# A two-layer transformer trunk: pairs of up-projection tiles as seven block products, and weight sums made by adding transfers

## The chip, the cores and the metric

The kernel runs on one core of a Trainium2 chip. The time is the device time of one execution in microseconds (us); less is better. The kernel before took 1202.36 us (median of three runs, 1201.91 to 1202.77).

The engines of the core are named as the profile names them: PE is TensorE (matmuls), PEld its weight loads, DVE is VectorE, ACT is ScalarE, POOL is GpSimd and SP is SyncE, which here only issues transfers. Each engine runs its own queue of instructions in order and waits on semaphores for what others have to finish first.

## The reference

x has 512 tokens of 1024 features. Each of two layers mixes tokens (an mLSTM in the first, pooling in the second), attends to a memory of 256 tokens, and ends with a squared-ReLU MLP of 4096 hidden features. The change touches only the MLP:

```python
ALPHA = (2 * DEPTH) ** 0.25                    # DEPTH = 2
def sq_relu_mlp(x, w1, b1, w2, b2):
    return jnp.square(jax.nn.relu(x @ w1 + b1)) @ w2 + b2
...
for i in range(DEPTH):
    ...
    x = layer_norm(ALPHA * x + sq_relu_mlp(x, mlp_w1[i], mlp_b1[i], mlp_w2[i], mlp_b2[i]),
                   ln_g[i, 2], ln_b[i, 2])
```

All of it is float32.

## The kernel before

**Split products.** Every float32 operand is kept as a high part (a copy rounded to the matmul's own float32 form) and a low part (what the rounding left). `mm3` (L196) makes one product of three matmuls: high by high, high by low, low by high. The parts of a weight tile are made by `unit` (L160, L161): ACT casts the raw 128x1024 tile to `wh`, DVE subtracts `wh` from it and writes `wl`. The pools hold five `wh`, five `wl` and eight large activation tiles.

**The MLP** goes in four quarters q of 1024 hidden features. In each, the up projection makes eight tiles h of 128 features by 512 tokens. `feat_tile` (L299) makes one of them with 8 x 3 matmuls that stream 512 columns of xm (the normalised x, transposed; `xm00h` and `xm01h` are the high parts of its first and last 512 features in layer 0, `xm10h` and `xm11h` in layer 1). `feat_first` (L287) makes the first four of q = 0 in two rounds of 256 columns, so that they can begin while the last tokens are still being normalised. ACT turns each tile into relu (r, L809) and its square (s, L810).

For q = 0, 1 and 2 `up_down` (L799) makes the down projection as seven block products instead of eight (Strassen's scheme in Winograd's form): the hidden features are cut into four blocks a11, a21, a12, a22, the weights into b11, b12, b21, b22; sums of blocks are formed, split into parts (`split`, L777 and L778; `weight_split`, L786 and L787), and `product` multiplies them in the PSUM banks u, f and m2. After each product `onto` (L845) adds a bank to x or subtracts it. `each` (L833) forms the weight sums t1, t2, t3, t4 on DVE, 128x1024 at a time. Just after `feat_first`, x is scaled and b2 is added (L820). Quarter q = 3 is done plainly.

**Order.** The program is written in the order of the code, and a list scheduler of the framework then orders the instructions of each engine by its own costs. Each engine runs its queue in that order.

Of the kernel before, what the change touches and what calls it, by code (L numbers as in the profile page):

```python
# [19 lines left out]
KC = D // P  # L20
# [13 lines left out]
SUM = sum(SEG)  # L34
WU = 1024
LN_T = 7.2


def f32(ap):
    return ap.bitcast(F32)  # L40
# [3 lines left out]
def trunk(ctx: ExitStack, tc: tile.TileContext, a: dict, out: bass.AP):  # L44
    nc = tc.nc
    V, A, G, T = nc.vector, nc.scalar, nc.gpsimd, nc.tensor
# [5 lines left out]
    act_p = pool("act", 8)  # L52
    wh_p = pool("wh", 5)
    wl_p = pool("wl", 5)
# [14 lines left out]
    scoped = {}  # L69
# [20 lines left out]
    def ld(dst, src):  # L90
        nc.sync.dma_start(dst, src)
# [561 lines left out]
    for i in range(DEPTH):  # L653
# [120 lines left out]
        def split(name, src):  # L774

            h, l = [scoped["hid"].tile([P, 4, 256], F32R, tag="hid", name=f"{name}{p}") for p in "hl"]
            A.copy(h, src)  # L777
            V.tensor_tensor(l, src, f32(h), ALU.subtract)  # L778
            return h, l

        def weight_split(name, src):
            us = []
            for j, r in enumerate(src):
                h = wh_p.tile([P, WU], F32R, tag="wh", name=f"{name}h{j}")
                l = wl_p.tile([P, WU], F32R, tag="wl", name=f"{name}l{j}")
                A.copy(h, r)  # L786
                V.tensor_tensor(l, r, f32(h), ALU.subtract)  # L787
                us.append([z.rearrange("p (k m) -> p k m", m=512) for z in (h, l)])
            return us

        def product(ps, lhs, rhs, start, evac):

            for g in range(2):
                for k in range(4):
                    w = rhs[k // 2]
                    mm3(ps[g], tuple(z[:, k, tok(g)] for z in lhs), (w[0][:, k % 2], w[1][:, k % 2]), start=start and k == 0, stop=k == 3, skip=not start)
                evac(g, ps[g])

        def up_down(q, n):  # L799
# [25 lines left out]
            def load(name, hf, j, z=None):  # L825
                z = z or [scoped["rawd"].tile([P, WU], F32, tag="rawd", name=f"{name}{n}{z}") for z in range(2)]
                for w in range(2):
                    ld(z[w], a["w2"][i, q, hf, j + w])
                return z

            def each(dst, x_, y_, op):
                for d, u, v in zip(dst, x_, y_):
                    V.tensor_tensor(d, u, v, op)  # L833

            for m in range(first, KC):
                ev(m, feat_tile(f"h{n}{m}", a["w1"][i, 8 * q + m], xm, aux_p, "aux"))
                if m == 3 or m == first == 4:
                    L["M1"] = split(f"a11{n}", a11)
                    V.tensor_tensor(a11, a11, a21, ALU.subtract)
                    L["M7"] = split(f"q3{n}", a11)  # L840
# [12 lines left out]
            b11 = load("b11", 0, 0)  # L853
            product(u, L["M1"], weight_split(f"b11{n}", b11), True, onto(0, 0))
            b12 = act_p.tile([P, 2, WU], F32, tag="act", name=f"b12{n}")
            b12 = load("b12", 1, 0, [b12[:, w] for w in range(2)])
            each(b11, b11, b12, ALU.add)
            V.tensor_tensor(a21, a21, a22, ALU.subtract)
            product(f, split(f"q1{n}", a21), weight_split(f"t1{n}", b11), True, onto(1, 1))
            b22 = load("b22", 1, 2)  # L860
            V.scalar_tensor_tensor(a11, a11, -1.0, a22, ALU.mult, ALU.subtract)
            each(b11, b11, b22, ALU.add)
            product(u, split(f"q2{n}", a11), weight_split(f"t2{n}", b11), False, onto(0, 1, ALU.subtract))
            b21 = load("b21", 0, 2)
            product(m2, split(f"a12{n}", a12), weight_split(f"b21{n}", b21), True, onto(0, 0))
            each(b12, b12, b22, ALU.add)
            product(u, L["M7"], weight_split(f"t3{n}", b12), False, onto(1, 1, ALU.subtract))
            V.tensor_tensor(a12, a12, a11, ALU.add)
            product(f, split(f"q4{n}", a12), weight_split(f"b22{n}", b22), False, onto(0, 1))
            each(b11, b11, b21, ALU.add)  # L870
            product(u, split(f"a22{n}", a22), weight_split(f"t4{n}", b11), False, onto(1, 0))

        for q in range(3):
            up_down(q, f"{i}{q}")
# [110 lines left out]
```

## Time and profile before

| of the profiled execution | |
|---|---|
| its own time | 1203.3 us |
| span from the first to the last instruction | 1201.2 us |
| PE busy | 1189.4 us, 99% of the span |
| DVE busy | 812.6 us, 68% |
| ACT busy | 575.5 us, 48% |
| mean granted TensorE clock | 0.998 of full speed |
| bytes moved | 146.58 MB |

The execution's own time is 2.1 us over its span. A matmul's row gives its length from start to modelled end; matmuls overlap, so what one costs is read from the distance between two starts. A letter such as `h<-xm00h,wh` means: writes h, reads xm00h and wh; the numbers of tiles are left out in rows of the trace. In the rows of the program's order the tile's own number stands behind its name: `h003` is feature tile 3 of layer 0, quarter 0, and `a1100h` is the high part of block a11 of layer 0, quarter 0.

### The profile page before, as it was taken

The page shows a single profiled execution, that of the slowest core. Times are in us where ns is not written, and L with a number is a line of the kernel's source. Part 1 is how long each engine was busy: PE and PEld are TensorE (multiplying, and loading weights), DVE is VectorE, ACT ScalarE, POOL GpSimd, SP SyncE. Part 2 cuts the span into 40 slices and gives each one's busy share as a digit, 9 for nine tenths or more (in the row PEclk, how much of TensorE's full clock was granted, in tenths as well). Part 3 has the DMA queues.
Part 4 walks back from the last instruction along what each step waited for, and adds up shares of the span by engine and source line. Part 5 has one row for each costly group of instructions (what it writes and reads, how often), then busy time and mean ns, then how long its engine had stood idle before and what let it go on. Part 6 is the DMA issues. An engine that isn't in the chain of part 4 may idle for free.

```text
span 1201.2 us, 15360 instructions
## 1 busy us (share of the span) xinstructions
PE 1189.4 (99%) x6105; PEld 1013.5 (84%) x6105; DVE 812.6 (68%) x1089; ACT 575.5 (48%) x832; POOL 19.1 (2%) x51
## 2 busy tenths in 40 slices
PE   9999999999999999999999999999999999999997
PEld 6888899889888988888888888998988888888886
DVE  6764466585549685693884598874968569388336
ACT  6685775224423553454545434552355445454530
POOL 0211000000000000000000000000000000000000
PEclk9999999999999999999999999999999999999999
DMA  7244257633243306125025355635231513502311
GB/s 270 95 136 123 88 158 263 199 100 107 70 162 101 124 21 207 53 99 181 1 67 216 123 193 176 185 115 175 88 123 39 189 53 118 163 1 73 103 53 70
DMA packets 44056, 146.58 MB, mean 122 GB/s; under 512 B 5568, under 2 KB 5836, under 8 KB 43984
## 3 DMA queue, kind: packets, MB, share of 16 engines
q1 hardware_dynamic: 42960, 142.96, 36.2%
q0 software_dynamic: 1024, 2.64, 1.0%
q8 instruction: 48, 0.79, 0.3%
q14 instruction: 24, 0.20, 0.0%
HBM read 139.27 MB, written 6.31 MB: 121 GB/s over the span
## 4 chain that ended last, share of the span: by engine, by line
PE 94%; DVE 2%; ACT 1%; DMA 1%; issue 0%; SPq 0%; DVEq 0%; ACTq 0%
PE h L198 10%; PE h L197 10%; PE h L199 10%; PE u L197 4%; PE u L198 4%; PE u L199 4%; PE m L197 3%; PE m L199 3%; PE m L198 3%; PE ao L199 2%; PE ao L197 2%; PE ao L198 2%; PE q L197 2%; PE q L198 2%; PE q L199 2%; PE f L199 2%
## 5 line engine op out<-in xcount | busy, mean ns | idle before, releaser
L161 DVE TENSOR_TENSOR wl<-raw,wh 128x1024 fp32r<-128x1024 f32 x175 | 213.3, 1221 | 194.0 <-ACT wh L160 192.0
L160 ACT CAST wh<-raw 128x1024 fp32r<-128x1024 f32 x175 | 183.3, 1050 | 286.5 <-PE h L198 92.1
L833 DVE TENSOR_TENSOR b<-b,b 128x1024 f32<-128x1024 f32 x48 | 57.6, 1220 | 0.4
L197 PE MATMUL h<-xm10h,wh 128*128 128x512 f32 (+1 forms) x144 | 52.8, 367 | 0.0
L197 PE MATMUL h<-xm00h,wh 128*128 128x512 f32 (+1 forms) x144 | 52.8, 367 | 0.0
L197 PE MATMUL h<-xm01h,wh 128*128 128x512 f32 (+1 forms) x144 | 52.8, 367 | 0.0
L197 PE MATMUL h<-xm11h,wh 128*128 128x512 f32 (+1 forms) x144 | 52.8, 367 | 0.0
L198 PE MATMUL h<-xm00l,wh 128*128 128x512 f32 (+1 forms) x144 | 52.7, 366 | 0.0
L198 PE MATMUL h<-xm10l,wh 128*128 128x512 f32 (+1 forms) x144 | 52.7, 366 | 0.0
L199 PE MATMUL h<-xm01h,wl 128*128 128x512 f32 (+1 forms) x144 | 52.6, 365 | 0.0
L199 PE MATMUL h<-xm10h,wl 128*128 128x512 f32 (+1 forms) x144 | 52.6, 365 | 0.0
L199 PE MATMUL h<-xm11h,wl 128*128 128x512 f32 (+1 forms) x144 | 52.6, 365 | 0.0
L199 PE MATMUL h<-xm00h,wl 128*128 128x512 f32 (+1 forms) x144 | 52.6, 365 | 0.0
L198 PE MATMUL h<-xm01l,wh 128*128 128x512 f32 (+1 forms) x144 | 52.6, 365 | 0.0
L198 PE MATMUL h<-xm11l,wh 128*128 128x512 f32 (+1 forms) x144 | 52.6, 365 | 0.0
L809 ACT ACTIVATE r<-h,b 128x512 f32<-128x512 f32 x48 | 32.8, 683 | 14.8 <-PE h L199 14.8
L248 ACT ACTIVATE rs<-mv,eps_t 128x1 f32<-128x1 f32 x24 | 7.1, 294 | 53.3 <-DVE mv L246 53.3
L810 ACT ACTIVATE s<-r 128x512 f32<-128x512 f32 x48 | 30.4, 633 | 1.5
L198 PEld LDWEIGHTS h<-xm10l,wh 128*128 128x128 f32 x144 | 27.2, 189 | 4.5
L198 PEld LDWEIGHTS h<-xm00l,wh 128*128 128x128 f32 x144 | 27.2, 189 | 4.4
L199 PEld LDWEIGHTS h<-xm00h,wl 128*128 128x128 f32 x144 | 27.2, 189 | 4.4
L197 PEld LDWEIGHTS h<-xm11h,wh 128*128 128x128 f32 x144 | 27.2, 189 | 4.4
(912 smaller groups left out, 3493.6 us busy)
## 6 DMA issues: line engine op xcount, KB each, us to landing
raw<-in_w SPq DMA_DIRECT2D x88, 512.0 KB, 3.8
b<-in_w SPq DMA_DIRECT2D x48, 512.0 KB, 4.5
raw<-in_w_q SPq DMA_DIRECT2D x24, 512.0 KB, 4.3
raw<-in_w_ao SPq DMA_DIRECT2D x16, 512.0 KB, 3.6
raw<-in_w_v SPq DMA_DIRECT2D x8, 512.0 KB, 6.0
raw<-in_w_o SPq DMA_DIRECT2D x8, 512.0 KB, 4.4
raw<-in_w_k SPq DMA_DIRECT2D x8, 512.0 KB, 4.2
raw<-in_w_kvv SPq DMA_DIRECT2D x8, 512.0 KB, 4.8
```

The source lines that it names most:

```text
L160: A.copy(h, r)
L161: V.tensor_tensor(l, r, f32(h), ALU.subtract)
L197: T.matmul(out_, l[0], r[0], start=start, stop=False, skip_group_check=skip)
L198: T.matmul(out_, l[0], r[1], start=False, stop=False, skip_group_check=skip)
L199: T.matmul(out_, l[1], r[0], start=False, stop=stop, skip_group_check=skip)
L248: A.activation(rs, mv[:, 1:2], AF.Sqrt, bias=eps_t, scale=1.0)
L809: A.activation(r, ps, AF.Relu, bias=b1[:, i, 8 * q + m : 8 * q + m + 1], scale=1.0)
L810: A.activation(s[m // 4][:, m % 4], r, AF.Square)
L833: V.tensor_tensor(d, u, v, op)
```

## The change

Three edits, all in the MLP of both layers.

1. **Pairs of up tiles.** `STRASSEN_UP` names, for q = 0, 1, 2, which pairs (m, m+1) of feature tiles are made by the new `up_pair`: two, three and three of four, 16 in all. A pair is a product of 256 features by 1024 inputs by 512 tokens. It is made of seven block products of 128 features, 512 inputs and 256 tokens (4 x 3 matmuls of 256 columns each, 84 in all), where two calls of `feat_tile` take 48 matmuls of 512 columns. Its weights come raw (u1, u2); DVE forms four sums of 128x512, and three 128x1024 tiles and one of 128x512 are split instead of two 128x1024. The seven products go to three PSUM banks (pa, pb, pc of 256 columns), and ACT and DVE put them together in s by copies and additions (four on ACT, four on DVE); relu and square then run in place on s.
2. **Sums of x.** `x_sums` runs once in each layer, in q = 0: DVE adds the parts of the four blocks of xm (xr..), forms the four sums q1 to q4 in that, and splits them (ACT casts, DVE subtracts). These are twelve passes of 128x1024 on DVE and four casts on ACT. In the code it stands after `first_blocks` (the split of a11 and of a11 - a21).
3. **Weight sums by transfers.** `each` is gone. t1, t2, t3, t4 are formed in place by transfers on POOL's queue that add what they read to the tile in SBUF (`onto_w`, `accum_op=ADD`): eight of 512 KB in each `up_down`, 48 in all, besides the eight plain loads that stay. Each waits until the tile's earlier contents have been split. The order of the seven products becomes M1, t1, b21, t2, t3, b22, t4.

```diff
+STRASSEN_UP = ((2, 3), (0, 1, 2), (0, 1, 2))
...
+        def x_sums():
...
+            r22, r21 = raw(1, 1), raw(1, 0)
+            r11 = raw(0, 0)
+            V.tensor_tensor(r11, r11, r21, ALU.subtract)
+            parts("q3", r11, act_p)
+            V.tensor_tensor(r21, r21, r22, ALU.subtract)
+            parts("q1", r21, act_p)
+            V.scalar_tensor_tensor(r11, r11, -1.0, r22, ALU.mult, ALU.subtract)
+            parts("q2", r11, scoped["hid"])
+            r12 = raw(0, 1)
+            V.tensor_tensor(r12, r12, r11, ALU.add)
+            parts("q4", r12, scoped["hid"])
+
+        def up_pair(q, m, n, s):
...
+            b11, b21 = hl("ub", u1)
+            V.tensor_tensor(ta[:, h2[0]], u1[:, h2[0]], u2[:, h2[0]], ALU.add)
+            V.tensor_tensor(tb[:, h2[0]], ta[:, h2[0]], u2[:, h2[1]], ALU.add)
+            V.tensor_tensor(tb[:, h2[1]], tb[:, h2[0]], u1[:, h2[1]], ALU.add)
+            t2_, t4 = hl("utb", tb)
+            V.tensor_tensor(ta[:, h2[1]], u2[:, h2[0]], u2[:, h2[1]], ALU.add)
+            t1, t3 = hl("uta", ta)
+            (b22,) = hl("ud", u2[:, h2[1]])
...
+            prod(pa, b11, block(0, 0), True)
+            A.copy(z1[:, lo], pa)
+            prod(pc, b21, block(0, 1), True)
+            V.tensor_tensor(z1[:, lo], z1[:, lo], pc, ALU.add)
+            prod(pa, t2_, xq["q2"], False)
+            A.activation(z2[:, lo], pa, AF.Copy, scale=-1.0)
+            prod(pb, t1, xq["q1"], True)
+            A.copy(z2[:, hi], pb)
+            prod(pa, t3, xq["q3"], False)
+            V.tensor_tensor(z2[:, hi], z2[:, hi], pa, ALU.subtract)
+            prod(pb, b22, xq["q4"], False)
+            V.tensor_tensor(z2[:, lo], z2[:, lo], pb, ALU.add)
+            prod(pa, t4, block(1, 1), False)
+            A.copy(z1[:, hi], pa)
+            for c, z in enumerate((z1, z2)):
+                A.activation(z, z, AF.Relu, bias=b1[:, i, 8 * q + m + c : 8 * q + m + c + 1], scale=1.0)
+                A.activation(z, z, AF.Square)
...
+            if q == 0:
+                first_blocks()
+                x_sums()
+            for m in range(first, KC, 2):
+                if m // 2 in STRASSEN_UP[q]:
+                    up_pair(q, m, n, s[m // 4])
+                else:
+                    for z in range(2):
+                        ev(m + z, feat_tile(f"h{n}{m + z}", a["w1"][i, 8 * q + m + z], xm, aux_p, "aux"))
+                if m == 2:
+                    first_blocks()
...
-            each(b11, b11, b12, ALU.add)
...
+            def onto_w(z, hf, j):
+
+                for w in range(2):
+                    G.dma_start(z[w], a["w2"][i, q, hf, j + w], accum_op=ALU.add)
+
+            b = load("b11", 0, 0)
+            w = weight_split(f"b11{n}", b)
+            onto_w(b, 1, 0)
+            product(u, L["M1"], w, True, onto(0, 0))
             V.tensor_tensor(a21, a21, a22, ALU.subtract)
-            product(f, split(f"q1{n}", a21), weight_split(f"t1{n}", b11), True, onto(1, 1))
...
+            w = weight_split(f"t1{n}", b)
+            onto_w(b, 1, 2)
+            product(f, split(f"q1{n}", a21), w, True, onto(1, 1))
```

What the change does to the order of three queues is shown at the places that the prediction speaks of, all in layer 0, q = 0.

On DVE, before, the last x rows (L820) are followed by the low parts of the four weight tiles of the single tiles h004 to h007 and by the parts of b11 and a11:

```order
L820 SCALAR_TENSOR_TENSOR xin3_2056<-xin3_2056,b20_3757 128x1024
L161 TENSOR_TENSOR wl68_3766<-raw68_3763,wh68_3765 128x1024
L161 TENSOR_TENSOR wl69_3809<-raw69_3806,wh69_3808 128x1024
L161 TENSOR_TENSOR wl70_3843<-raw70_3840,wh70_3842 128x1024
L161 TENSOR_TENSOR wl71_3877<-raw71_3874,wh71_3876 128x1024
L787 TENSOR_TENSOR b1100l0_3919<-b11000_3914,b1100h0_3918 128x1024
L778 TENSOR_TENSOR a1100l_3798<-s000_3495,a1100h_3797 128x1024
```

On DVE, in the change, twelve passes on the weights of two pairs (tiles 4 and 5, and 6 and 7) stand behind the last x row, and then this stretch, in which L822 writes the low parts of x's sums:

```order
L850 TENSOR_TENSOR ub006wl_3929<-up006_3922,ub006wh_3928 128x1024
L779 TENSOR_TENSOR a1100l_3764<-s000_3495,a1100h_3763 128x1024
L850 TENSOR_TENSOR utb006wl_3936<-ut006b_3927,utb006wh_3935 128x1024
L924 TENSOR_TENSOR s000_3495<-s000_3495 128x4x256
L779 TENSOR_TENSOR q300l_3769<-s000_3495,q300h_3768 128x1024
L812 TENSOR_TENSOR xr011_3772<-xm01h_3386,xm01l_3387 128x1024
L812 TENSOR_TENSOR xr010_3774<-xm00h_3374,xm00l_3375 128x1024
L812 TENSOR_TENSOR xr000_3776<-xm00h_3374,xm00l_3375 128x1024
L827 TENSOR_TENSOR xr000_3776<-xr000_3776,xr010_3774 128x1024
L829 TENSOR_TENSOR xr010_3774<-xr010_3774,xr011_3772 128x1024
L822 TENSOR_TENSOR xq30_3779<-xr000_3776,xq30_3779 128x1024
L822 TENSOR_TENSOR xq10_3783<-xr010_3774,xq10_3783 128x1024
```

The sums of x have come between the end of `feat_first` and the rest of the quarter, behind the split of a11 and of q3, which need the last tile of `feat_first`.

On PE, before, the last matmul of `feat_first` (h003) is followed by the 512-column matmuls of h004:

```order
L199 MATMUL h003_3524<-xm01h_3386,wl67_3518 128x256
L197 MATMUL h004_3769<-xm00h_3374,wh68_3765 128x512
L198 MATMUL h004_3769<-xm00l_3375,wh68_3765 128x512
L199 MATMUL h004_3769<-xm00h_3374,wl68_3766 128x512
L197 MATMUL h004_3769<-xm00h_3374,wh68_3765 128x512
```

In the change it is followed by 36 matmuls of 256 columns that read xm alone (12 of the pair's first product, ua004, 12 of the second, uc004, and 12 of the other pair's second, uc006), and then by this:

```order
L199 MATMUL uc006_3950<-xm01l_3387,ub006wh_3928 128x256
L200 MATMUL uc006_3950<-xm01h_3386,ub006wl_3929 128x256
L198 MATMUL ub004_3825<-xq10_3783,uta004wh_3816 128x256
L198 MATMUL ua006_3948<-xm00h_3374,ub006wh_3928 128x256
L199 MATMUL ua006_3948<-xm00l_3375,ub006wh_3928 128x256
```

The 37th matmul reads xq1, a sum of x, and everything else of PE's queue stands behind it.

On ACT, before, at the down projection's first two weight sums t1 and t2, the cast of t200h0 waits for sums that DVE makes, and q100h, the block that the first f product reads, follows three rows later:

```order
L786 CAST t100h0_3962<-b11000_3914 128x1024
L786 CAST t100h1_3966<-b11001_3915 128x1024
L809 ACTIVATE r006_3871<-h006_3846,b1_985 128x512
L810 ACTIVATE s001_3496<-r006_3871 128x512
L786 CAST t200h0_4007<-b11000_3914 128x1024
L809 ACTIVATE r007_3905<-h007_3880,b1_985 128x512
L810 ACTIVATE s001_3496<-r007_3905 128x512
L777 CAST q100h_3958<-s000_3495 128x1024
```

In the change the same casts stand so, each `t..` cast now behind a transfer that adds to its tile:

```order
L787 CAST t100h0_4093<-b11000_4052 128x1024
L887 ACTIVATE s001_3496<-s001_3496,b1_985 128x512
L888 ACTIVATE s001_3496<-s001_3496 128x512
L885 COPY s001_3496<-ua006_3948 128x256
L787 CAST t100h1_4097<-b11001_4053 128x1024
L887 ACTIVATE s001_3496<-s001_3496,b1_985 128x512
L787 CAST b2100h0_4141<-b21000_4133 128x1024
L888 ACTIVATE s001_3496<-s001_3496 128x512
L787 CAST b2100h1_4145<-b21001_4134 128x1024
L787 CAST t200h0_4182<-b11000_4052 128x1024
L778 CAST q100h_4103<-s000_3495 128x1024
```

q100h, which the first f product reads, still stands behind t200h0, and t200h0 now behind two adding transfers one after the other.

## Rows read from the trace of the kernel before

**Rows 1.** The page's head: span, busy time of each engine, granted clock in forty slices.

```profile
span 1201.2 us, 15360 instructions
PE 1189.4 (99%) x6105; PEld 1013.5 (84%) x6105; DVE 812.6 (68%) x1089; ACT 575.5 (48%) x832; POOL 19.1 (2%) x51
PEclk9999999999999999999999999999999999999999
```

**Rows 2.** The page's chain that ended last, by engine.

```profile
PE 94%; DVE 2%; ACT 1%; DMA 1%; issue 0%; SPq 0%; DVEq 0%; ACTq 0%
```

**Rows 3.** PE's waits, the longest two: total, times, longest, in us.

```profile
PE warm L311 <- POOL zero L308: 1.3, 1, 1.3
PE po L199 <- DVE d1l L207: 1.1, 1, 1.1
```

**Rows 4.** Busy time by stretch (us, engines in turn, then clock, DMA share, GB/s).

```profile
378.00:403.40 25.40, 25.40 (x212) 25.18 (x211) 19.27 (x24) 10.84 (x16) 0.00 (x0) 1.00 0.60 185
403.40:425.20 21.80, 21.80 (x99) 18.04 (x98) 15.56 (x13) 11.01 (x15) 0.00 (x0) 1.00 0.22 73
```

**Rows 5.** PE's timeline from `feat_first`'s last tile to the down projection.

```profile
397.64 0.28 PE L197 MATMUL h<-xm00h,wh 128*128 128x256 f32 x1
...
403.28 0.28 PE L199 MATMUL h<-xm01h,wl 128*128 128x256 f32 x1
403.40 0.40 PE L197 MATMUL h<-xm00h,wh 128*128 128x512 f32 x1
...
425.19 0.39 PE L197 MATMUL u<-b1100h,a1100h 128*128 128x512 f32 x1
```

**Rows 6.** DVE's timeline: the last x row and the first work behind it.

```profile
391.37 1.22 DVE L820 SCALAR_TENSOR_TENSOR xin<-xin,b 128x1024 f32<-128x1024 f32 x1
392.51 1.22 DVE L161 TENSOR_TENSOR wl<-raw,wh 128x1024 fp32r<-128x1024 f32 x1
```

**Rows 7.** DVE's timeline: passes one right behind the other.

```profile
430.38 1.22 DVE L778 TENSOR_TENSOR q100l<-s,q100h 128x1024 fp32r<-128x1024 f32 x1
431.51 0.68 DVE L845 TENSOR_TENSOR xin<-xin,u 128x512 f32<-128x512 f32 x1
432.11 1.22 DVE L778 TENSOR_TENSOR q200l<-s,q200h 128x1024 fp32r<-128x1024 f32 x1
```

**Rows 8.** ACT's timeline at the end of `feat_first`.

```profile
403.48 1.05 ACT L786 CAST b1100h<-b 128x1024 fp32r<-128x1024 f32 x1 [0.58 <-PE h L198]
404.44 0.68 ACT L809 ACTIVATE r<-h,b 128x512 f32<-128x512 f32 x1
405.15 0.64 ACT L810 ACTIVATE s<-r 128x512 f32<-128x512 f32 x1
405.82 1.05 ACT L777 CAST a1100h<-s 128x1024 fp32r<-128x1024 f32 x1
```

**Rows 9.** Groups by line: busy time, mean ns of one, idle time before.

```profile
L161 DVE TENSOR_TENSOR wl<-raw,wh 128x1024 fp32r<-128x1024 f32 x175 | 213.3, 1221 | 194.0 <-ACT wh L160 192.0
L833 DVE TENSOR_TENSOR b<-b,b 128x1024 f32<-128x1024 f32 x48 | 57.6, 1220 | 0.4
L207 DVE TENSOR_TENSOR vl<-v,vh 128x256 fp32r<-128x256 f32 x16 | 6.7, 419 | 9.1 <-ACT vh L206 9.0
L209 ACT ACTIVATE q11h<-q 128x256 fp32r<-128x256 f32 x8 | 3.1, 384 | 4.8 <-PE q L199 4.8
```

**Rows 10.** DMA issues: size of each, median us from issue to landing.

```profile
b<-in_w SPq DMA_DIRECT2D x48, 512.0 KB, 4.5
...
w<-rows POOLq DMA_DIRECT2D x4, 256.0 KB, 3.6
...
wpr<-in_w_pool SPq DMA_DIRECT2D x2, 512.0 KB, 9.7
...
w<-rows POOLq DMA_DIRECT2D x4, 64.0 KB, 3.3
```

**Rows 11.** Busy time by stretch at the program's start: the warm-up matmuls of 512 columns.

```profile
1.30:5.50 4.20, 4.18 (x9) 2.81 (x9) 0.69 (x1) 1.96 (x3) 0.56 (x6) 1.00 0.78 250
```

More of the change, by code (lines that the diff above doesn't have):

```diff
@@ L797, in product, with block, raw, parts @@
                 evac(g, ps[g])
+        xq = {}
+        def block(r, c):
+            return xm.half(c, slice(256 * r, 256 * r + 256))
+        def x_sums():
+            def raw(r, c):
+                z = scoped["hid"].tile([P, 4, 256], F32, tag="hid", name=f"xr{i}{r}{c}")
+                h, l = block(r, c)
+                V.tensor_tensor(z, f32(h), f32(l), ALU.add)
+                return z
+            def parts(name, src, pool_):
+                if pool_ is act_p:
+                    z = act_p.tile([P, 2, 4, 256], F32R, tag="act", name=f"x{name}{i}")
+                    h, l = z[:, 0], z[:, 1]
+                else:
+                    h, l = [pool_.tile([P, 4, 256], F32R, tag="hid", name=f"x{name}{i}{p}") for p in "hl"]
+                A.copy(h, src)
+                V.tensor_tensor(l, src, f32(h), ALU.subtract)
+                xq[name] = h, l
+            r22, r21 = raw(1, 1), raw(1, 0)
[9 more added lines that the diff above has]
+            parts("q4", r12, scoped["hid"])
@@ new lines, in up_pair, with hl, prod @@
+        def up_pair(q, m, n, s):
+            src = [a["w1"][i, 8 * q + m + z] for z in range(2)]
+            h2 = slice(0, 512), slice(512, 1024)
+            u1, u2 = [raw_p.tile([P, WU], F32, tag="raw", name=f"up{n}{m + z}") for z in range(2)]
+            ld(u1, src[0])
+            ld(u2, src[1])
+            ta, tb = [scoped["rawd"].tile([P, WU], F32, tag="rawd", name=f"ut{n}{m}{z}") for z in "ab"]
+            def hl(name, r):
+                h, l = [p.tile([P, WU], F32R, tag=t, name=f"{name}{n}{m}{t}")[:, : r.shape[1]] for p, t in ((wh_p, "wh"), (wl_p, "wl"))]
+                A.copy(h, r)
+                V.tensor_tensor(l, r, f32(h), ALU.subtract)
+                return [tuple(z[:, c].rearrange("p (k m) -> p k m", m=P) for z in (h, l)) for c in h2[: r.shape[1] // 512]]
+            b11, b21 = hl("ub", u1)
[6 more added lines that the diff above has]
+            (b22,) = hl("ud", u2[:, h2[1]])
+            pa = acc_p.tile([P, 512], F32, tag="acc", name=f"ua{n}{m}")[:, :256]
+            pb = acc_p.tile([P, 512], F32, tag="acc", name=f"ub{n}{m}")[:, :256]
+            pc = aux_p.tile([P, 512], F32, tag="aux", name=f"uc{n}{m}")[:, :256]
+            z1, z2 = s[:, m % 4], s[:, m % 4 + 1]
+            lo, hi = slice(0, 256), slice(256, 512)
+            def prod(ps, w, x_, start):
+                for k in range(4):
+                    mm3(ps, (w[0][:, k], w[1][:, k]), (x_[0][:, k], x_[1][:, k]), start=start and k == 0, stop=k == 3, skip=not start)
+            prod(pa, b11, block(0, 0), True)
[15 more added lines that the diff above has]
+                A.activation(z, z, AF.Square)
@@ L823, in up_down, with load @@
             L, R = {}, {}
-            def load(name, hf, j, z=None):
-                z = z or [scoped["rawd"].tile([P, WU], F32, tag="rawd", name=f"{name}{n}{z}") for z in range(2)]
+            def load(name, hf, j):
+                z = [scoped["rawd"].tile([P, WU], F32, tag="rawd", name=f"{name}{n}{z}") for z in range(2)]
                 for w in range(2):
@@ L829, in load, with first_blocks @@
                 return z
[L831 to L840, printed above, removed]
+            def first_blocks():
+                L["M1"] = split(f"a11{n}", a11)
+                V.tensor_tensor(a11, a11, a21, ALU.subtract)
+                L["M7"] = split(f"q3{n}", a11)
+            if q == 0:
[4 more added lines that the diff above has]
+                    up_pair(q, m, n, s[m // 4])
+                else:
+                    for z in range(2):
+                        ev(m + z, feat_tile(f"h{n}{m + z}", a["w1"][i, 8 * q + m + z], xm, aux_p, "aux"))
+                if m == 2:
+                    first_blocks()
             def onto(row, hf, op=ALU.add):
@@ L852, in up_down @@
             u, f, m2 = banks("u", acc_p, "acc"), banks("f", acc_p, "acc"), banks("m2", tmp_p, "tmp")
[L853 to L856, printed above, removed]
-            each(b11, b11, b12, ALU.add)
-            V.tensor_tensor(a21, a21, a22, ALU.subtract)
-            product(f, split(f"q1{n}", a21), weight_split(f"t1{n}", b11), True, onto(1, 1))
@@ L860, in up_down @@
-            b22 = load("b22", 1, 2)
[L861 to L867, printed above, removed]
+            def onto_w(z, hf, j):
+                for w in range(2):
+                    G.dma_start(z[w], a["w2"][i, q, hf, j + w], accum_op=ALU.add)
@@ new lines, in up_down @@
+            b = load("b11", 0, 0)
+            w = weight_split(f"b11{n}", b)
+            onto_w(b, 1, 0)
+            product(u, L["M1"], w, True, onto(0, 0))
+            V.tensor_tensor(a21, a21, a22, ALU.subtract)
+            w = weight_split(f"t1{n}", b)
+            onto_w(b, 1, 2)
+            product(f, split(f"q1{n}", a21), w, True, onto(1, 1))
+            b21 = load("b21", 0, 2)
+            l12 = split(f"a12{n}", a12)
+            product(m2, l12, weight_split(f"b21{n}", b21), True, onto(0, 0))
@@ L868, in up_down @@
+            t3 = load("t3", 1, 0)
+            onto_w(t3, 1, 2)
+            V.scalar_tensor_tensor(a11, a11, -1.0, a22, ALU.mult, ALU.subtract)
+            w = weight_split(f"t2{n}", b)
+            onto_w(b, 0, 2)
+            product(u, split(f"q2{n}", a11), w, False, onto(0, 1, ALU.subtract))
+            product(u, L["M7"], weight_split(f"t3{n}", t3), False, onto(1, 1, ALU.subtract))
+            b22 = load("b22", 1, 2)
             V.tensor_tensor(a12, a12, a11, ALU.add)
             product(f, split(f"q4{n}", a12), weight_split(f"b22{n}", b22), False, onto(0, 1))
-            each(b11, b11, b21, ALU.add)
@@ L871, in up_down @@
-            product(u, split(f"a22{n}", a22), weight_split(f"t4{n}", b11), False, onto(1, 0))
+            product(u, split(f"a22{n}", a22), weight_split(f"t4{n}", b), False, onto(1, 0))
         for q in range(3):
```

## The prediction

> **What bounds the kernel now.** I read the page's head first: PE is busy for 1189.4 of 1201.2 us, DVE for 812.6, ACT for 575.5, and the granted clock is full in every slice [rows 1]. The chain of work that ended last is PE's for 94% [rows 2], and PE's longest waits are 1.3 and 1.1 us [rows 3]. So matmul time taken away comes off the end, DVE time does not, and each wait made for PE adds in full. The stretch at the change shows it: from 378.00 to 425.20 PE is busy to the last hundredth, while DVE has 6.1 and 6.2 us of idle in the two windows [rows 4].
>
> The profiled execution took 1203.3 us; the median is 1202.36, so I take 0.9 off at the end. About 0.2%, 2.4 us, is what a measurement of this kernel can tell from no change.
>
> **Term A, the matmuls.** A matmul's cost is the distance between starts. `feat_tile`'s 96 of 512 columns run from 403.40 to 425.19, 0.227 each; `feat_first`'s last 48 of 256 columns from 397.64 to 403.40, 0.120 each [rows 5]. Half the columns cost more than half. A pair costs 84 x 0.120 = 10.08 where it cost 48 x 0.227 = 10.90, so it saves 0.82, and 16 pairs save **13.1 us**. At exactly half, 0.1135, they would save 21.8; the row with 256 columns is the operation itself, so I take 0.120.
>
> **Term B, the sums of x.** These are DVE work that PE waits for, at a place where DVE has none to spare. When `feat_first` ends at 403.40, PE finds 36 matmuls that read xm alone, 36 x 0.120 = 4.3 us, until 407.7. The 37th reads xq1.
>
> DVE's queue up to xq1: it comes to the first pair at 392.51. Passes one behind the other start 1.14 apart at 1024 elements (391.37 to 392.51) [rows 6] and 0.60 at 512 (431.51 to 432.11) [rows 7]. The thirteen passes on the pairs' weights that stand first (four of 1024, nine of 512) are 4 x 1.14 + 9 x 0.60 = 10.0 us of work; with the casts that they wait for, which stand on ACT behind relu and square of each tile, I let them end about 403.7, under `feat_first`. Then DVE stands before a1100l, whose high part ACT can cast only after the last tile of `feat_first`: the last matmul ends at 403.28 + 0.28 = 403.56 [rows 5], relu and square take 0.71 and 0.67 from start to start, the cast 1.05 [rows 8], so 406.1. From there: a11's low part, utb006, a11 - a21 are three passes, to 409.5; ACT casts q3 in 1.05, to 410.6; then q3's low part, three raw adds (L812) and two differences (L827, L829) are six passes of 1.14, with the last one's tail to 417.9; ACT casts xq1 in 1.05, to 419.0. PE waits from 407.7 to 419.0, **11.3**. The queue behind holds the low part of xq1 (0.65 more after the few matmuls that don't need it), xq2's high part (0.9) and its low part (0.25). Together 13.1 in each layer, **+26.2 us**; the bounds are 11.3 if those last three hide, and 14. The cover that could hide it, other matmuls, isn't there: PE's queue is in order.
>
> **Term C, the adding transfers.** No row shows one. In q = 0 q100h, which the first f product needs, stands behind t200h0 on ACT. From b11's cast the chain is: cast 1.05, low part 1.22, a transfer A, cast 1.05, low part 1.22, a second transfer A, t200h0's cast 1.05 and q100h's 1.05, some 6.7 + 2A with the hand-overs [rows 8, 9]. PE has meanwhile 59 matmuls of 256 columns and 24 of 512, 59 x 0.120 + 24 x 0.227 = 12.5. The wait is 2A - 5.8. Bounds for A: the least, 3.3, is a 64 KB transfer on POOL's queue, the most 9.7, the slowest of 512 KB; nearer are 3.6 (256 KB, POOL's queue) and 4.5 (512 KB of these weights, SP's queue) [rows 10]. I take 5, a little over the 4.5, since an adding transfer also has to read the tile. That gives 4.2 a layer, **+8.4 us**; with 3.3 it is 0.8 a layer, with 9.7 it is 13.6. In q = 1 and 2 the f product has 72 x 0.227 + 25 x 0.120 = 19.3 us of PE work ahead, and there t201h0 and t202h0 stand behind the q1 blocks, so nothing shows unless A is over about 8. Queued behind each wait on ACT are evictions of the pairs, on POOL only the next adding transfers. SP's queue issues as many loads as before; the DMA engines are busy for 0.22 in this stretch [rows 4], so the added bytes have room.
>
> The Trainium skill speaks against this edit ("Collectives: The Full Stack", why ReduceScatter is half of AllGather): an add in a DMA engine reads two sources, two descriptors for each chunk, and runs at half the rate of a copy. With its price for a transfer on this queue ("DMA: Bandwidth & Descriptors", Anatomy of one DMA: 2.0 us and bytes over 436 GB/s) 512 KB would land in 3.2 us, by an estimate 4.4 with the read doubled, and the sum would be 1226; the trace takes 3.6 for half the bytes where that price says 2.6, so it doesn't agree, and nothing shown has an adding transfer.
>
> **Term D, the clock.** After standing for 11 us PE may not be at full speed. The only long-idle start in the trace is the program's own: nine warm-up matmuls of 512 columns took 4.18 us, 0.46 each [rows 11], twice the 0.227 of later ones, so 2.1 us were lost there, although that row prints a granted clock of 1.00. Two such restarts, one in each layer, are **+4.2 us**; bounds 0 and 8.8, if half speed lasts twice as long.
>
> The Trainium skill ("TensorE: Matmul & The Clock Gate") has an idle PE fall to half clock; its consequence would be the same 0.46 for a matmul, which the row on the warm-up agrees with in size but not in the printed clock.
>
> **Edits at nothing.** The 48 DVE adds of `each`, 57.6 us [rows 9], go; PE's waits are elsewhere [rows 3], so nothing comes off. A steady pair asks of DVE 3.5 x 1.14 + 4 x 0.60 + 4 evictions of 256 columns at 0.34 (0.419 less the overlap of 0.08) = 7.8 [rows 7, 9], of ACT 3.5 x 0.96 + 4 x 0.29 (0.384 less an overlap of 0.09) + 2 x 1.38 for relu and square = 7.3 [rows 8, 9], both under PE's 10.08. If an eviction is late, PE waits for the bank: an exposed 0.42 for 48 of the pairs' hand-overs would be 20 us, the bound for a rival below.
>
> **Sum.** 1203.3 - 13.1 + 26.2 + 8.4 + 4.2 = 1229.0, less 0.9: **1228 us**, 2.1% slower.
>
> **The rivals.**
> - *Adding transfers are slow (A of 8 and over).* For it: an add must read what it writes, and the slowest 512 KB row is 9.7. Against it: the common rows are 3.3 to 4.5. At 8 term C is 20.4 and the time 1240; at 9.7 it is 27.2, with some 2 us at each of the four quarters q = 1 and 2 about 35, and the time 1255; 1262 with the upper bounds of B and D in part.
> - *Pairs are not hidden.* A product of 12 matmuls lasts 1.4 us, and three banks serve seven products, so each next product on a bank waits until a copy of 0.384 or an add of 0.419 has read it [rows 9]. For it: the margin between two products on one bank is a single product. Against it: ACT and DVE have 2.8 and 2.3 us to spare in each pair by the sums above. Some 16 of the 20 us would give 1244, between 1235 and 1250.
> - *The other side: faster.* x's sums come before PE needs them. It decides at 13.1 us of savings: both waits together would have to be under 6.5 us in a layer. The sums read only xm, finished by about 391, so the data would allow it; but the queue puts them behind a1100l, and nine passes at 1.14 alone are 10.3 against a cover of 4.3. They would have to take about half of what every row shows, with C and D at nothing. With waits of 3 us a layer the time is 1203.3 - 13.1 + 6 - 0.9 = 1195; the range of this case is 1189 (no wait) to 1200.
> - *No change.* Waits and savings cancel: B would have to be half of what the queue gives, 6.5 a layer, with C and D at nothing.
>
> **How the numbers follow.** The forecast, terms A to D at their likely values, has 0.62 and its own range is 1214 (B at 11.3, A at 3.4, no clock loss: 1203.3 - 13.1 + 22.6 + 2 - 0.9 = 1213.9) to 1243 (A of 8 or D at its upper bound in part). Slow adding transfers have 0.20, exposed pairs 0.12, faster 0.04, no change 0.02. Predicted is the forecast's 1228. The range is 1212 to 1262: it takes in the forecast, the exposed pairs and the slow transfers, and leaves out the last two and the tails. Slower by over 0.2% has 0.62 + 0.20 + 0.12 = 0.94.
>
> **What would show it.** A: starts 0.120 apart in the pairs, and PE's busy time lower by about 13 us. B: one wait of PE of 11 us in each layer just after `feat_first`, put down to ACT's cast of xq1 (L821), with DVE busy through it. C: a wait of PE at the first f product of q = 0, put down to q100h or t100h0, and a landing time of about 5 us for 512 KB on POOL's queue; none at q = 1 and 2. D: matmuls 0.46 or 0.24 apart for some us behind the first wait. Wrong would be: no wait of several us at xq1, which would throw out the queue's order as I read it; or waits at every pair, on ACT or DVE reading pa, pb or pc.

## The result and the profile after

The changed kernel takes 1238.11 us (median of five runs, 1236.16 to 1240.52) where the kernel before takes 1202.36: a ratio of 1.0299, with a 95% interval of 1.0281 to 1.0316. The profiled execution took 1239.97 by its own time, 36.7 more than the one of before.

The page of the changed kernel, its head and its chain that ended last:

```profile
span 1238.2 us, 16983 instructions
...
PE 1188.6 (96%) x6681; PEld 1037.9 (84%) x6681; DVE 869.7 (70%) x1209; ACT 627.4 (51%) x936; POOL 62.2 (5%) x99
...
PEclk9999999999999789999999999999988999999999
...
q0 software_dynamic: 7936, 27.81, 12.9%
...
PE 85%; DVE 5%; DMA 4%; ACT 3%; issue 1%; SPq 0%; POOL 0%; DVEq 0%; ACTq 0%; POOLq 0%
```

Against [rows 1] and [rows 2]: PE is as busy as before to 0.8 us in a span 37 us longer, so nearly all that was added is waiting, and DVE, DMA and ACT have a larger part of the chain. The clock drops in two places, a third and three quarters of the way through: q = 0 of each layer. PE's waits, which were 1.3 and 1.1 at the most [rows 3], say the same:

```profile
PE ub L198 <- ACT xq L821: 23.8, 2, 11.9
PE f L198 <- ACT q110h L778: 7.4, 1, 7.4
PE f L198 <- ACT q100h L778: 6.9, 1, 6.9
```

PE's timeline at the first wait shows the 36 matmuls of xm running out (the last one ends at 407.72), the wait, and a slow stretch behind it, with starts 0.21 to 0.22 apart until 424, then 0.12:

```profile
407.44 0.28 PE L200 MATMUL uc<-xm01h,ub006wl 128*128 128x256 f32 x1
419.62 0.58 PE L198 MATMUL ub<-xq,uta004wh 128*128 128x256 f32 x1 [11.90 <-ACT xq L821]
420.00 0.41 PE L198 MATMUL ua<-xm00h,ub006wh 128*128 128x256 f32 x1
420.22 0.41 PE L199 MATMUL ua<-xm00l,ub006wh 128*128 128x256 f32 x1
...
424.21 0.28 PE L199 MATMUL ua<-xm00l,ub006wh 128*128 128x256 f32 x1
424.33 0.28 PE L200 MATMUL ua<-xm00h,ub006wl 128*128 128x256 f32 x1
```

DVE's timeline through that wait is the queue that the prediction walked: a11's low part at 406.74 behind its cast, then, but for 1.11 us in which DVE waits for the cast of q3, nearly without a gap to the two differences (the second is shown); ACT casts xq1 at 418.52 (first row of the next fence):

```profile
406.74 1.23 DVE L779 TENSOR_TENSOR a1100l<-s,a1100h 128x1024 fp32r<-128x1024 f32 x1 [1.11 <-ACT a1100h L778]
...
417.27 1.22 DVE L829 TENSOR_TENSOR xr<-xr,xr 128x1024 f32<-128x1024 f32 x1
```

ACT's timeline, there and at the second wait, where the casts of t1 and t2 stand behind the adding transfers:

```profile
418.52 1.04 ACT L821 CAST xq<-xr 128x1024 fp32r<-128x1024 f32 x1 [0.21 <-DVE xr L829]
...
440.28 1.05 ACT L787 CAST t100h<-b 128x1024 fp32r<-128x1024 f32 x1 [4.21 <-DMA b<-in_w]
...
448.57 1.04 ACT L787 CAST t200h<-b 128x1024 fp32r<-128x1024 f32 x1 [1.21 <-DMA b<-in_w]
449.52 1.04 ACT L778 CAST q100h<-s 128x1024 fp32r<-128x1024 f32 x1
```

POOL's timeline: the two transfers that these casts wait for are issued when the low parts before them are written. From issue to cast they take 6.4 and 5.6 us:

```profile
433.86 0.88 POOL L953 DMA_DIRECT2D b<-in_w  x1 [1.32 <-DVE s L883]
...
442.99 0.86 POOL L953 DMA_DIRECT2D b<-in_w  x1 [6.29 <-DVE t100l L788]
```

DMA issues, with the median us to landing (against [rows 10]):

```profile
b<-in_w POOLq DMA_DIRECT2D x36, 512.0 KB, 6.0
...
t<-in_w POOLq DMA_DIRECT2D x12, 512.0 KB, 6.7
```

Three windows of layer 0: behind the first wait, behind the second, and one after (the granted clock is the column behind POOL's):

```profile
419.62:424.10 4.48, 4.48 (x20) 4.36 (x21) 3.70 (x5) 1.64 (x3) 0.00 (x0) 0.50 0.02 4
...
450.60:454.70 4.10, 4.09 (x10) 3.23 (x11) 4.10 (x4) 1.49 (x2) 0.00 (x0) 0.50 0.70 266
454.70:458.00 3.30, 3.30 (x16) 2.71 (x15) 2.19 (x3) 1.22 (x2) 0.88 (x1) 0.98 0.25 22
```

**Where the 36.7 us are.** The first matmul of each f product marks a quarter. PE's timeline of before and then of the change, layer 0, q = 0, 1, 2:

```profile
430.63 0.39 PE L197 MATMUL f<-t100h,q100h 128*128 128x512 f32 x1
...
512.47 0.39 PE L197 MATMUL f<-t101h,q101h 128*128 128x512 f32 x1
...
594.32 0.39 PE L197 MATMUL f<-t102h,q102h 128*128 128x512 f32 x1
```

```profile
450.61 0.80 PE L198 MATMUL f<-t100h,q100h 128*128 128x512 f32 x1 [6.87 <-ACT q100h L778]
...
532.59 0.39 PE L198 MATMUL f<-t101h,q101h 128*128 128x512 f32 x1
...
612.40 0.39 PE L198 MATMUL f<-t102h,q102h 128*128 128x512 f32 x1
```

Up to the first mark the change has lost 20.0 us. The step from the first mark to the second is 81.98 (before 81.84), from the second to the third 79.81 (before 81.85). So a steady quarter with three pairs gains 2.04, 0.68 a pair; in layer 1 the same step is 79.69 for 81.84, 0.72 a pair. The first step contains the slow clock behind f, and has lost 2.2 against the second (3.1 in layer 1, where the clock is 0.51 in the 6.09 us from 947.21). Behind xq the slow clock took 2.2 in layer 0 (half of the 4.48 us) and 1.5 in layer 1 (the clock is 0.66 in the 4.50 us from 916.00). The account: waits for xq 23.8, waits at f 14.3, slow clock 2.2 + 1.5 behind xq and 2.2 + 3.1 behind f, together 47.1; less 16 pairs at 0.70, 11.2: 35.9 of the 36.7. The four pairs of q = 0 are counted at the price of the others. This says where PE's time lies; it doesn't say what comes back if one item is taken away.

### The profile page after: what moved, and what is told of

The parts are those of the page before. It is cut to its first block, busy times and chain, and to the rows that moved or that the text cites. A ratio compares the mean times of both kernels' runs of the same rounds, so it can differ in the third digit from the quotient of the medians.

```text
span 1238.2 us, 16983 instructions
## 1 busy us (share of the span) xinstructions
PE 1188.6 (96%) x6681; PEld 1037.9 (84%) x6681; DVE 869.7 (70%) x1209; ACT 627.4 (51%) x936; POOL 62.2 (5%) x99
## 3 DMA queue, kind: packets, MB, share of 16 engines
q0 software_dynamic: 7936, 27.81, 12.9%
## 4 chain that ended last, share of the span: by engine, by line
PE 85%; DVE 5%; DMA 4%; ACT 3%; issue 1%; SPq 0%; POOL 0%; DVEq 0%; ACTq 0%; POOLq 0%
PE h L199 4%; PE h L198 4%; PE h L200 4%; PE m L198 3%; PE m L200 3%; PE m L199 3%; PE u L199 3%; PE u L198 3%; PE u L200 3%; DMA b<-in_w 3%; PE ao L198 2%; PE ao L200 2%; PE ao L199 2%; PE q L198 2%; PE q L199 2%; PE q L200 2%
## 5 line engine op out<-in xcount | busy, mean ns | idle before, releaser
L162 DVE TENSOR_TENSOR wl<-raw,wh 128x1024 fp32r<-128x1024 f32 x143 | 174.2, 1220 | 129.7 <-ACT wh L161 127.6
L161 ACT CAST wh<-raw 128x1024 fp32r<-128x1024 f32 x143 | 149.5, 1048 | 203.3 <-PE h L199 40.3
L953 POOL DMA_DIRECT2D b<-in_w x36 | 31.6, 879 | 148.7 <-DVE t210l L788 13.3
L198 PE MATMUL h<-xm00h,wh 128*128 128x512 f32 (+1 forms) x80 | 27.9, 349 | 0.0
L199 PE MATMUL h<-xm10l,wh 128*128 128x512 f32 (+1 forms) x80 | 27.8, 348 | 0.0
L199 PE MATMUL h<-xm00l,wh 128*128 128x512 f32 (+1 forms) x80 | 27.8, 348 | 0.0
L200 PE MATMUL h<-xm01h,wl 128*128 128x512 f32 (+1 forms) x80 | 27.7, 347 | 0.0
L200 PE MATMUL h<-xm11h,wl 128*128 128x512 f32 (+1 forms) x80 | 27.7, 347 | 0.0
L199 PE MATMUL h<-xm01l,wh 128*128 128x512 f32 (+1 forms) x80 | 27.7, 347 | 0.0
L199 PE MATMUL h<-xm11l,wh 128*128 128x512 f32 (+1 forms) x80 | 27.7, 347 | 0.0
L198 PE MATMUL k<-memh,wh 128*128 128x256 f32 x64 | 18.5, 289 | 0.0
L198 PE MATMUL q<-xa10h,wh 128*128 128x256 f32 x64 | 18.5, 289 | 0.0
```

Source lines behind the costliest of these rows:

```text
L953: G.dma_start(z[w], a["w2"][i, q, hf, j + w], accum_op=ALU.add)
```

## The experiments

Each ratio is to the kernel before, run on the same chip.

**The sums late, no pairs in q = 0.**

```diff
-STRASSEN_UP = ((2, 3), (0, 1, 2), (0, 1, 2))
+STRASSEN_UP = ((), (0, 1, 2), (0, 1, 2))
...
             if q == 0:
                 first_blocks()
-                x_sums()
...
                 if m == 2:
                     first_blocks()
+            if q == 0:
+                x_sums()
```

> The sums of x are written behind the up tiles of q = 0 and the pairs of q = 0 are single tiles again (12 pairs in place of 16); adding transfers kept. Theory (the place in DVE's queue makes the wait): PE's two waits of 11.9 us for xq go, and with them the half-clock stretch behind each (21 matmuls at 0.213 for 0.120, 2.0 us); the f product of q = 0 has single tiles ahead of it again, so its wait falls from 6.9 to under 3 and its half-clock stretch goes too. 1238.1 - 23.8 - 4.0 - 14.3 + (0 to 6) - 4.0 + 4 x 0.82 = 1195 to 1201. Rival (DVE has no room for 13.7 us of passes anywhere in q = 0): a wait of several us appears at the products of q = 0 or at the first pair of q = 1, and the time stays over 1215.

Measured 1201.65 us, ratio 1.0 (0.9989 to 1.0011). The waits for xq are gone and no other took their place; those at f fell to 2.1 in each layer:

```profile
PE f L198 <- ACT q110h L778: 2.1, 1, 2.1
PE f L198 <- ACT q100h L778: 2.1, 1, 2.1
```

The rival's 1215 is out. The time is 0.65 above the range that I expected: a good part of what 12 pairs save goes to f, whose first product starts at 433.14, 2.5 later than before.

**Weight sums by DVE again, pairs and sums of x as in the change.**

```diff
-            onto_w(b, 1, 0)
+            b12 = load("b12", 1, 0)
+            each(b11, b11, b12, ALU.add)
...
+            b21 = load("b21", 0, 2)
+            product(m2, l12, weight_split(f"b21{n}", b21), True, onto(0, 0))
+            each(b11, b11, b21, ALU.add)
-            product(u, split(f"a22{n}", a22), weight_split(f"t4{n}", b), False, onto(1, 0))
+            product(u, split(f"a22{n}", a22), weight_split(f"t4{n}", b11), False, onto(1, 0))
```

The order of the products changes with it: t2 and t3 follow t1, and b21 stands just before t4.

> The change, but the weight sums are formed by DVE from loaded tiles as before (b12 in the pool of the other weight tiles; the b21 product stands before the last one for it); pairs and sums of x as in the change. Theory (the adding transfers make the wait at f): the two waits of 6.9 and 7.4 us at f go, and the half-clock stretch of about 2.1 us behind each: 1238.1 - 14.3 - 4.2 = 1219.6, with up to 3 more for DVE's adds beside the pairs; the waits for xq stay at 11.9. Rival (DVE is what q = 0 lacks, and eight more passes of 1.14 in it move the wait to t1 or t2): PE waits of 5 us and more at f or u in q = 0, time 1230 or more.

Measured 1228.77, ratio 1.022 (1.0202 to 1.0237), 9.3 under the change where I expected 18.5; it lies between the range of the theory and that of the rival. The first f product starts at 443.56, 7.1 earlier, with a wait of 0.36, so the waits at f go with the transfers:

```profile
443.56 0.50 PE L198 MATMUL f<-t100h,q100h 128*128 128x512 f32 x1 [0.36 <-ACT q100h L778]
```

Part of what comes back is DVE's. The windows from there have the clock at full and DVE without a free moment:

```profile
443.00:456.00 13.00, 12.12 (x50) 9.04 (x49) 13.00 (x14) 5.48 (x6) 0.00 (x0) 1.00 0.00 0
456.00:470.00 14.00, 13.78 (x61) 11.39 (x62) 14.00 (x16) 7.63 (x9) 0.00 (x0) 1.00 0.23 76
```

PE loses 1.1 us there in small pieces. The step to the second mark is 83.68, 1.7 over the change's although that one has the slow clock in it. Another 1.5 us of PE's idle time lie between 470 and 527, where DVE is busy for 49.55 of 57.00 us and three of PE's waits (0.8, 0.4 and 0.3) are put down to ACT. Each theory had half: the transfers make the wait at f, and with the eight passes back DVE is full behind it; how much of the rest is DVE's was not tried apart.

**Adding transfers alone** (`STRASSEN_UP` with three empty rows, no `x_sums`).

> Adding transfers alone: no pairs and no sums of x. Theory (the wait at f is two landings against the PE work ahead of f): single tiles leave some 20 us of PE work between b11's cast and f where the chain is 6.7 + 2 x 6.3 = 19.3, so there is no wait: 1202.4, within 2.4 of the kernel before. Rival (the transfers are slow in themselves, or crowd out the loads): waits at f or u in all six quarters, 2 us and more each, 1212 or more.

Measured 1202.08, ratio 0.9998 (0.9989 to 1.0007): no change. DVE's 57.6 us [rows 9] leave and nothing comes off, as predicted; PE has no wait at f. This third edit costs nothing where the single tiles cover it.

**The transfers overwrite,** so that the weight sums are left out.

```diff
-                    G.dma_start(z[w], a["w2"][i, q, hf, j + w], accum_op=ALU.add)
+                    G.dma_start(z[w], a["w2"][i, q, hf, j + w])
```

> The change, but the 48 transfers on POOL's queue overwrite the tile instead of adding to it: the same bytes and the same waits, the weight sums are not formed. Theory (the add's second read makes the landing long): landing falls from 6.0 and 6.7 to about 4.5, the wait at f from 6.9 to 6.9 - 2 x 1.7 = 3.5, in both layers: 1238.1 - 7 = 1231, or 1227 if the clock then stays up behind it. Rival (POOL's queue is slow whatever it moves): landing stays at 6 or over and the time within 2.4 of the change.

Measured 1232.37, ratio 1.0249 (1.0233 to 1.0264). The page, its waits and its DMA issues:

```profile
PE f L198 <- ACT q110h L778: 3.6, 1, 3.6
PE f L198 <- ACT q100h L778: 3.3, 1, 3.3
```

```profile
q0 software_dynamic: 7936, 27.81, 7.5%
...
b<-in_w POOLq DMA_DIRECT2D x36, 512.0 KB, 3.9
...
t<-in_w POOLq DMA_DIRECT2D x12, 512.0 KB, 4.7
```

Without the add the same bytes land in 3.9 in place of 6.0 and take 7.5% of the engines' time in place of 12.9%. The wait at f falls by 3.6 in layer 0 and by 3.8 in layer 1. That is the add's own price. The Trainium skill ("Collectives: The Full Stack", why ReduceScatter is half of AllGather) says of a collective's add that it needs two source reads, which brings ReduceScatter to half of AllGather's rate. The queue had 1.0% in the kernel before, so the 48 transfers take 11.9% for 6.5%, 1.8 times as much: for these transfers the trace nearly agrees. The landing is 1.5 times as long.

**q1 split before t1's weights,** on top of the first experiment.

```diff
+            V.tensor_tensor(a21, a21, a22, ALU.subtract)
+            lq1 = split(f"q1{n}", a21)
             product(u, L["M1"], w, True, onto(0, 0))
-            V.tensor_tensor(a21, a21, a22, ALU.subtract)
             w = weight_split(f"t1{n}", b)
```

> As the run with the sums late, and q1 is split before t1's weights, so that on ACT q100h no longer stands behind t200h0 and f waits for one adding transfer, not two. Theory (what ate that run's gain is f's wait, 2.1 us a layer, and the slow clock behind it): the wait at f falls under 1 us, and 12 pairs at 0.70 show: 1201.6 - 2 x (1.2 to 2.1) - up to 1.6 = 1196 to 1199, faster than the kernel before by 0.3 to 0.5%. Rival (the pairs themselves save nothing, their evictions and splits eat it): within 0.2% of 1202.

Measured 1199.57, ratio 0.9974 (0.9964 to 0.9983). The waits at f's first matmul are 0.7 in each layer and those for its low part 0.5. It is faster than before, but 0.6 above the expected range: the sums of x, late, still stand ahead of t1's split on DVE (where a later run puts them first, f has no wait in q = 0).

**The sums first** (`x_sums()` written ahead of `first_blocks()`, else the change).

> The change with one line moved: the sums of x are written ahead of the split of a11, not behind it, so they stand right behind the last x row in DVE's queue (16 pairs, adding transfers kept). Theory (place in the queue): xq1 is ready near 402, before PE asks; the wait moves to the first pair's own weights, whose split now stands behind the sums: 14 passes of 1.14 and four of 0.60 from 392.4 are 410.8 against 406.1 for PE, so 3 to 6 us in place of 11.9; f's wait stays. 1238.1 - 2 x 7.4 - 2 x 2 = 1219 (1214 to 1225). Rival (the amount of DVE work sets the wait wherever the sums stand): waits of 10 us and over in the first pairs, 1233 or more.

Measured 1226.53, ratio 1.0193 (1.0179 to 1.0207). No wait for xq is left in the list. DVE writes xq1's low part at 402.65 and the pair's own weights come late instead:

```profile
402.65 1.22 DVE L822 TENSOR_TENSOR xq<-xr,xq 128x1024 fp32r<-128x1024 f32 x1
...
410.80 1.22 DVE L850 TENSOR_TENSOR uta004wl<-ut004a,uta004wh 128x1024 fp32r<-128x1024 f32 x1
```

Those waits are 4.8 us in all in layer 0 (2.3, 1.2 and four of 0.3 to 0.4) in place of 11.9. f starts at 443.97 for 450.61. The time is 1.5 over my upper edge. I had taken 2 us of slow clock a layer off, and most of it stayed: behind waits of 2.3 and 0.4 us the clock is 0.58 from 424 to 428. f's waits stay, at 5.6 and 7.8, as expected.

**Four pairs in q = 1 and 2,** on top of the first experiment.

> As the run with the sums late, but all four pairs in q = 1 and 2, 16 in all. Theory (an adding transfer's chain needs cover before f, and a pair at the end of the quarter takes 10.1 us where the two tiles with their early-known weights gave more room): waits of 3 to 8 us and slow clock behind them at f in the four quarters: 1201.6 - 2.8 + 4 x 5 to 9 = 1215 to 1235. Rival (a pair more is only 0.7 us less): 1198.8, no new waits.

Measured 1244.09, ratio 1.0335 (1.0308 to 1.0363), slower than any other and 9 over my upper edge. PE's waits, and ACT's timeline at the first of them:

```profile
PE f L198 <- ACT q101h L778: 8.2, 1, 8.2
PE f L198 <- ACT q102h L778: 8.1, 1, 8.1
PE f L198 <- ACT q112h L778: 7.4, 1, 7.4
```

```profile
517.11 1.04 ACT L787 CAST t101h<-b 128x1024 fp32r<-128x1024 f32 x1 [3.96 <-DMA b<-in_w]
...
522.48 1.04 ACT L778 CAST q101h<-s 128x1024 fp32r<-128x1024 f32 x1
```

The fourth wait is 7.4 as well. The last two tiles of a quarter as single tiles cover the adding transfers: with a pair there, PE comes to f 11.7 us after b11's second cast begins (503.68 to 515.34), in the change's q = 1 17.1 us after (515.53 to 532.59). The waits are as long as those of q = 0 in the change, but the chain is another: q101h stands behind the second half of t1 and behind b21, not behind t2, so it is one transfer deep. That half's transfer was issued at 509.69, 3.7 us after the low part it waits for was written, and took 7.4 us to the cast. What held its issue the rows don't show.

**PE kept busy in the first wait.**

```diff
+            def keep(z):
+                ps = tmp_p.tile([P, 512], F32, tag="tmp", name=f"keep{i}")
+                for n in range(10):
+                    T.transpose(ps[:, tok(n % 4)], z[:, n % 4, :P], ident)
...
+            keep(r22)
...
+            keep(r21)
...
```

> The change, and in the wait for xq1 PE transposes what DVE has just written, into a bank that nobody reads (60 transposes of 128 columns in each layer). Theory (the wait costs its length and then a stretch at half clock): the first product still starts near 419.6, and from there matmuls of 256 columns start 0.120 apart, not 0.213: 1238.1 - 2 x 2.0 to 2.3 = 1233.7. Rival (the slow stretch is memory or weight loads catching up, not the engine's idling): spacing stays at 0.213 for some 20 matmuls and the time within 1 of the change.

Measured 1241.85, ratio 1.0326 (1.031 to 1.0341). PE's timeline:

```profile
417.21 2.55 PE L828 MATMUL keep<-ident,xr 128*128 128x128 f32 x20 [0.84 <-DVE xr L835]
419.53 0.39 PE L198 MATMUL ub<-xq,uta004wh 128*128 128x256 f32 x1
419.75 0.28 PE L198 MATMUL ua<-xm00h,ub006wh 128*128 128x256 f32 x1
419.87 0.28 PE L199 MATMUL ua<-xm00l,ub006wh 128*128 128x256 f32 x1
...
423.00 0.38 PE L198 MATMUL ua<-xq20h,utb004wh 128*128 128x256 f32 x1 [0.28 <-ACT xq20h L821]
424.22 0.38 PE L198 MATMUL ub<-xq,uta006wh 128*128 128x256 f32 x1 [0.83 <-ACT uta006wh L859]
```

The mechanism is as I held: starts are 0.12 apart from 419.75 on, the idling was the cause of the slow stretch. The gain is not, 8 us short of my 1233.7: PE then runs into xq2 and uta006, which DVE and ACT bring no sooner. b11's first cast begins at 430.63 in place of 431.12, so of the 2.2 us behind the first wait at most 0.5 reach the next chain; its first adding transfer then takes 7.6 us to the cast where the change's took 6.4, and f starts at 451.31 after a wait of 8.05, 0.7 later than in the change. Most of the half speed behind the first wait was hidden under the rest of DVE's queue; between the two waits DVE, ACT and the transfers set the time, not PE.

**The sums first, no pairs in q = 0, q1 first,** and **the change without its pairs in q = 0.** The first takes `x_sums()` ahead of `first_blocks()`, the empty first row of `STRASSEN_UP` and the split of q1 as above; the second alters only that row.

> The sums of x right behind the last x row, single tiles in q = 0, pairs in q = 1 and 2 (12), adding transfers, q1 split before t1's weights. Theory (each part of the loss was a place in a queue): no wait for xq, and with the sums out of the way of t1's split f's wait goes as well; 12 pairs at 0.70 show whole: 1202.4 - 8.4 = 1194, 1193 to 1196, faster than the kernel before by 0.5 to 0.8%. Rival (the sums only move the wait to the single tiles of q = 0, whose low parts now stand behind twelve passes of DVE): waits of 2 us and more at h in q = 0, 1198 or more.

> The change with one number row altered: no pairs in q = 0 (12 in all), the sums of x where the change has them. Theory (the wait for xq exists because q = 0 itself uses the sums at once): nothing asks for xq before q = 1, the wait goes although the sums stand where they stood; f waits some 2 us in each layer since DVE's sums stand ahead of t1's split: 1202.4 - 8.4 + 2 x (2 + 1) + 1 = 1199 to 1202. Rival (the sums' place behind a11 delays PE whoever uses them): waits over 5 us in q = 0, 1212 or more.

Measured 1195.56, ratio 0.9951 (0.9937 to 0.9964), and 1198.97, ratio 0.9968 (0.9958 to 0.9978). The first lies in the expected range, the second at its lower edge. In the first, PE doesn't wait for f's first matmul (two waits of 0.6 and 0.4 for a low part are left, one each in q = 2 and q = 1); the first mark lies where that of before lies, and then the quarters are 80.08 and 80.04 us for 81.85:

```profile
430.38 0.39 PE L198 MATMUL f<-t100h,q100h 128*128 128x512 f32 x1
...
510.46 0.39 PE L198 MATMUL f<-t101h,q101h 128*128 128x512 f32 x1
...
590.50 0.50 PE L198 MATMUL f<-t102h,q102h 128*128 128x512 f32 x1
```

In the second the sums stand in the code where the change has them, and no wait for xq appears: what counts is that q = 0 itself asks for them. f's waits there are 0.9 in each layer, and q1's place was not changed. So the idea gains 0.3 to 0.5% where its preparation has a quarter's time, and loses 3% where it has 4.3 us.

## Why the prediction was right

It was right in sign and cause, and 10 us short in size: 1228 forecast, 1238.11 measured, inside the likeliest case's own range of 1214 to 1243. The time alone would not have told the forecast from two rivals (slow transfers 1240, exposed pairs 1235 to 1250); the waits and the landings do.

- **Term A** was 13.1; the quarter steps give 0.70 a pair, not 0.82, so 11.2. The price of a matmul held: 0.120 between starts. What the sum left out are short waits at the hand-over from one product to the next. In the three pairs between the second and the third mark PE's starts are 0.12 apart but at two such places: 574.00, 574.25 and 574.47 (ub to ua), and 578.54, 578.69 and 578.92 (uc to ua), together some 0.4 us. The sign that I gave, 13 us less of PE's busy time, didn't come: it fell by 0.8, since at half clock the same matmuls are busy for longer. In the run with 12 pairs and no slow clock (1195.56) it fell by 8.5, 0.71 a pair.
- **Term B** was 26.2, measured 23.8. The wait was forecast from 407.7 to 419.0 and stood from 407.72 to 419.62. That is closer than my own rows were: from 410.6, six passes of 1.14 end with the last one's tail at 417.5, not 417.9, and xq1's cast at 418.5. I also had the last relu begin as `feat_first` ends (403.40 here), but ACT's cast of ub006's high part stands first and it begins at 404.28; the two slips partly cancel. The 1.8 us a layer behind it (xq1's low part, xq2) didn't show as waits, because PE was then at half clock and came to them late. With PE kept busy xq2's high part shows again, as 0.28, and uta006, which I had not listed, as 0.83.
- **Term C** was 8.4, measured 14.3. The formula was right and A mis-sized: I took 5, by the 512 KB rows of SP's queue, and it is 6.0, because the add lengthens a landing of 3.9 by 2.1. 2 x 6.0 - 5.8 is 6.2; the waits were 6.9 and 7.4. In layer 0 the two transfers took 6.4 and 5.6, and the rest of the chain 7.4 where I had 6.7. That the added bytes have room was wrong: I read 0.22 off the kernel before, and in the change the DMA engines' share is 1.02 from 433.86 to 440.28, with the adding transfers issued at 431.65, 433.86 and 435.82 in flight. By the shares above one of them takes about 3.1 us of all 16 engines (11.9% of 1238.2 us for 48), a plain one 1.7, an estimate. The estimate of 4.4 worked out from the Trainium skill ("DMA: Bandwidth & Descriptors", Anatomy of one DMA) was further off; its price for a plain transfer, 3.2, stands against 3.9. As forecast, q = 1 and 2 had no such wait; with four pairs they had, by another chain.
- **Term D** was 4.2, for two restarts behind xq; these took 3.7 (2.2 and 1.5). It missed that the waits at f drop the clock as well, for another 5.3: by PE's rows there were four restarts, 9.0 in all, over the term's upper bound of 8.8 (which by its own 2.1 would be 8.4). The size of one was read from the warm-up, whose row prints a clock of 1.00, so that it came out near is partly luck. Those behind xq hardly lengthen the path: the experiment that took away the first wait's slow stretch gained nothing.
- **Edits at nothing:** the DVE adds taken away gained nothing (1202.08 with the transfers alone), and pairs with a whole quarter behind them are hidden but for that 0.12 a pair. A pair has three additions on DVE, not the four that I counted, so a steady pair asks of it 7.4 us, not 7.8.

Of the rivals, the slow transfers were not it (A is 6.0, not 8), nor were exposed pairs. The faster case named its condition rightly, both waits together under 6.5 us a layer: with the sums first and the pairs of q = 0 kept, 10.4 us of waits are left in layer 0 and the time is 1226.53; with those pairs given up, q1 first and no wait in q = 0 it is 1195.56.

What stays open: which engine's lateness makes the short waits in a pair was not tried apart, no run took the slow clock behind f away while leaving the wait, and the 0.8 us that the account leaves over has no row. The run of 1195.56 differs from that of 1198.97 in two things, the sums' place and q1's; q1's place alone was tried only with the sums late (ratios 1.0 and 0.9974).

## What to carry to other kernels

A product with fewer multiplications pays by its steady price only where its operands' sums are ready; ask which engine makes them, what stands ahead of them in its queue, and how much work of the bound engine covers that, at the first place that uses them and not on average. Two transfers in a chain, each waiting for the last reader of its tile, cost two landings, here 6 us each, and where several are in flight the DMA engines are full (1.02): an engine with much free time can do the same sums with less latency, if it has that time at the place. Waits that lie behind each other on the same chain are not added up freely: in the one run that tried it, speeding PE between them gave nothing.

## What the runs showed that was not expected

- An adding transfer of 512 KB lands in 6.0 us (median) where a plain one on the same queue takes 3.9, and 27.81 MB take 12.9% of the DMA engines' time in place of 7.5%.
- The length of a wait didn't tell what the slow clock (0.50, the lower of its two levels) behind it cost. In layer 0 a wait of 11.9 us was followed by a loss of 2.2 us and one of 6.9 by 2.1; in layer 1 one of 11.9 by 1.5, and one of 7.4 by 3.0.
- Half speed between two waits on one chain cost little or nothing.
